# Moving the elimination steps of three of four 32x32 inverses from VectorE to GpSimd

## The chip, the cores and the metric

The kernel runs on one core of a Trainium2 chip. A core has a matrix engine (TensorE, "PE" in the profile, with its weight loads as "PEld"), VectorE ("DVE"), ScalarE ("ACT"), GpSimd ("POOL") and SyncE ("SP"), which here only issues DMAs. Each engine works through its own queue in order; semaphores tie the queues together. The metric is the device time of one execution in microseconds, as the median of several runs.

## The reference

A decoder trunk of two layers on 272 tokens (16 learned ones and 256 given) of width 2048, in float32. The first layer mixes tokens with RWKV-7, the second with gated linear attention; a squared-ReLU MLP follows each. The change lies in the RWKV-7 recurrence, which the reference computes token by token, for 32 heads with a 64x64 state each:

```python
def step(S, inp):
    r_t, w_t, k_t, v_t, a_t, b_t = inp
    sa = jnp.einsum('bhvk,bhk->bhv', S, a_t)
    S = S * w_t[:, :, None, :] + sa[..., None] * b_t[:, :, None, :] + v_t[..., None] * k_t[:, :, None, :]
    y = jnp.einsum('bhvk,bhk->bhv', S, r_t)
    return S, y
```

## The kernel before

Activations lie transposed, features on the partitions. Every matrix product with weights runs as three passes of TensorE on rounded parts of the float32 values: a weight block of 1024 columns is loaded by SyncE (`wload`, L140), rounded to `hi` by ScalarE (L149), and VectorE takes the difference `lo = raw - hi` (L150); `mm3` (L172 to L174) multiplies. In the recurrence `wload` works in two halves of 512 columns. Two sets of `hi` and `lo` are in use at a time.

The recurrence works in chunks: 4 of 64 tokens and a last one of 16 (padded to 32), for two groups `g` of 16 heads. Inside a chunk the tokens depend on each other through a unit triangular system per head. A 64x64 system is cut into two 32x32 diagonal blocks and the block between them; the diagonal blocks are inverted, and `merge` (L1101) joins two of them with two small products on TensorE (L1110 and L1120). `invert(b)` inverts the 32x32 blocks of half a group at once, one system to a partition: `b` = 0 and 1 for the chunks 0, 1 and then 2, 3, 4 of the first group, `b` = 2 and 3 the same for the second. So four inverses follow each other. The even ones use 64 partitions (2 chunks x 2 blocks x 16 heads), the odd ones 128 (partitions 64 to 95 are zeros).

The way of one inverse: `scores(b, c, e)` (L930) makes the systems on TensorE (L940), VectorE masks them on their way out of PSUM into `AM` (the helper `tt`, line L703), SyncE sends the blocks to `sysd` in HBM (L947) and reads them back into `sysA`, one system to a partition (L966). GpSimd fills the diagonal with ones (L967; for odd `b` L963 clears the idle partitions). Then come 30 steps, `s` = 1 to 30, each a product into the small tile `upd` of `s` rows by `31 - s` columns and a sum into `sysA`: 60 instructions on VectorE, each waiting for the one before. `upd` has one buffer. After them SyncE stores `sysA` into `invd` (L977) and reads it back into `AM` in the layout of the chunks (L984), and VectorE transposes it into the spare partitions 64 to 95 of `sysA` (L979), from where L1110 reads it. L1120 reads the blocks that L984 brings.

Four things set the order of work here. TensorE's order is written out by hand: inside `tc.manual_schedule(engines={ENG.PE})` it takes the instructions as the program gives them. `R(n)` puts n units (three or so matmuls) of the value and output projections between the pieces of the recurrence, `until(n)` as many as are missing to n in all, `GAPS` and `MARK` are tables of such numbers, and `some(inv, n)` advances the generator `invert` by n yields. Nothing in TensorE's order looks at whether an inverse is done; when its turn comes, a merge waits. The other engines' orders come from the framework's planner, which replays the program with costs of its own and fills each queue by due priority; `tc.high_priority` moves loads and the stores around the inverse forward. VectorE's queue holds, beside the steps, the splits L150, the masks of the scores, the group norm of the first group (`norm`, L1263 to L1266, during the third inverse) and the additions of projection results to `r` and `hres`. GpSimd's queue holds in this part of the kernel only the fills, the copies of `WC` (L1054) and the clearing of `uv` for the last chunk (L1139).

## Time and profile before

| | |
|---|---|
| median of 3 runs | 2339.26 us (2339.04 to 2339.55) |
| the profiled execution | 2338.97 us, its span 2337.2 us |
| granted TensorE clock | 0.998 |
| recurrence with the four inverses | about 258 to 485 us of the span |
| inverses (first step to last, on VectorE) | 258.3 to 302.5, 328.1 to 353.7, 389.9 to 424.9, 439.1 to 474.2 us |

The span is the time between the first and the last instruction of the program; the execution's own time has a start and an end around it. A row of an engine with an instruction gives its duration; a "wait" is idle time of an engine put down to what ended it. Helpers record all their instructions under their own line: each `tt` of the recurrence stands under L703, so rows are told apart by the tiles they write and read, and `upd` and `sysA` mark the inverse.

### The profile page before, as it was taken

To read this page: it belongs to the slowest core of one execution; us is meant where nothing else is said; L and a number is where in the kernel's file an instruction comes from. 1 tells how busy PE (TensorE), PEld (TensorE's weight loads), DVE (VectorE), ACT (ScalarE), POOL (GpSimd) and SP (SyncE) were. 2 spreads that over 40 slices of the span, in tenths; PEclk is the share of its full clock that TensorE was granted. 3 is DMA by queue.
4 is the path that set the end of the run, shared out by engine and by line. 5 is a ranking of instruction groups with operands and counts; after the bars stand their busy time and mean duration, and the time that the engine had idled before them with its cause. 6 is when DMAs were issued, how large, how long until landed. Compare 5 with 4: busy or idle time off the path is not lost.

```text
span 2337.2 us, 49049 instructions
## 1 busy us (share of the span) xinstructions
PE 2308.0 (99%) x19183; PEld 2175.8 (93%) x19183; DVE 1816.0 (78%) x2979; ACT 1378.0 (59%) x2167; POOL 301.4 (13%) x597
## 2 busy tenths in 40 slices
PE   9999999999999999999999999999999999999998
PEld 8888888889999999999999999999998888898987
DVE  8868986848677667767767787677768989989877
ACT  6488645556555445445445565455577777777766
POOL 0000000000144444444430011000000000000000
PEclk9999999999999999999999999999999999999999
DMA  6459754535799999999996665555557777877875
GB/s 213 161 193 310 246 169 141 153 90 172 257 314 334 314 318 325 325 323 320 330 319 227 198 227 199 175 174 182 209 196 263 272 271 265 274 266 265 274 267 188
DMA packets 200326, 567.75 MB, mean 243 GB/s; under 512 B 41184, under 2 KB 56800, under 8 KB 199968
## 3 DMA queue, kind: packets, MB, share of 16 engines
q1 hardware_dynamic: 173216, 476.53, 59.7%
q0 software_dynamic: 26880, 88.10, 12.1%
q8 instruction: 151, 2.47, 0.4%
q14 instruction: 79, 0.65, 0.1%
HBM read 504.38 MB, written 58.46 MB: 241 GB/s over the span
## 4 chain that ended last, share of the span: by engine, by line
PE 83%; DVE 10%; ACT 3%; issue 2%; DMA 1%; SPq 0%; DVEq 0%; ACTq 0%
PE pj L172 16%; PE pj L174 16%; PE pj L173 16%; PE pj L418 10%; PE pj L419 5%; PE pj L205 2%; DVE lo L150 2%; PE pj L206 1%; PE pu L498 1%; PE pu L500 1%; PE pu L499 1%; PE pt L500 1%; PE pt L498 1%; PE pt L499 1%; ACT hi L149 1%
## 5 line engine op out<-in xcount | busy, mean ns | idle before, releaser
L149 ACT CAST hi<-raw 128x1024 fp32r<-128x1024 f32 (+1 forms) x562 | 526.1, 947 | 593.9 <-PE pj L173 530.6
L150 DVE TENSOR_TENSOR lo<-raw,hi 128x1024 fp32r<-128x1024 f32 (+1 forms) x562 | 613.1, 1100 | 224.8 <-ACT hi L149 220.1
L172 PE MATMUL pj<-x,hi 128*128 128x272 f32 (+1 forms) x2560 | 728.4, 285 | 2.0 <-DVE r L703 0.9
L174 PE MATMUL pj<-x,lo 128*128 128x272 f32 (+1 forms) x2560 | 714.7, 279 | 4.4 <-DVE lo L150 4.1
L173 PE MATMUL pj<-x,hi 128*128 128x272 f32 (+1 forms) x2560 | 713.6, 279 | 0.0
L172 PEld LDWEIGHTS pj<-x,hi 128*128 128x128 f32 x2560 | 484.8, 189 | 14.8 <-issue 6.5
L174 PEld LDWEIGHTS pj<-x,lo 128*128 128x128 f32 x2560 | 484.9, 189 | 6.8 <-DVE lo L150 6.5
L173 PEld LDWEIGHTS pj<-x,hi 128*128 128x128 f32 x2560 | 485.0, 189 | 2.5 <-issue 1.4
L372 DVE TENSOR_TENSOR lo<-raw,hi 128x1024 fp32r<-128x1024 f32 x364 | 405.1, 1140 | 72.1 <-ACT hi L664 70.8
L664 ACT CAST hi<-raw 128x1024 fp32r<-128x1024 f32 x364 | 352.3, 981 | 112.6 <-PE pj L418 30.7
L418 PE MATMUL pj<-x,hi 128*128 128x512 f32 x1024 | 339.5, 383 | 0.0
L172 PE MATMUL pj<-h,hi 128*128 128x272 f32 x1024 | 285.7, 279 | 0.0
L173 PE MATMUL pj<-h,hi 128*128 128x272 f32 x1024 | 285.7, 279 | 0.0
L174 PE MATMUL pj<-h,lo 128*128 128x272 f32 x1024 | 285.7, 279 | 0.0
L419 PE MATMUL pj<-x,lo 128*128 128x256 f32 x1024 | 279.2, 273 | 0.0
L418 PEld LDWEIGHTS pj<-x,hi 128*128 128x128 f32 x1024 | 193.5, 189 | 26.7
L419 PEld LDWEIGHTS pj<-x,lo 128*128 128x128 f32 x1024 | 196.4, 192 | 1.9 <-DVE lo L372 0.2
L172 PEld LDWEIGHTS pj<-h,hi 128*128 128x128 f32 x1024 | 193.5, 189 | 0.0
L173 PEld LDWEIGHTS pj<-h,hi 128*128 128x128 f32 x1024 | 193.5, 189 | 0.0
L174 PEld LDWEIGHTS pj<-h,lo 128*128 128x128 f32 x1024 | 193.5, 189 | 0.0
L358 POOL DMA_DIRECT2D diff<-x x168 | 90.2, 543 | 14.3 <-DVE x L351 5.1
L344 POOL DMA_DIRECT2D x<-w_d x168 | 89.8, 540 | 0.3
(359 smaller groups left out, 3517.7 us busy)
## 6 DMA issues: line engine op xcount, KB each, us to landing
raw<-mlp_w_d SPq DMA_DIRECT2D x384, 512.0 KB, 6.1
raw<-gla_in_d SPq DMA_DIRECT2D x98, 512.0 KB, 3.3
x<-w_d POOLq DMA_DIRECT2D x168, 256.0 KB, 6.8
diff<-x POOLq DMA_DIRECT2D x168, 256.0 KB, 8.6
raw<-w_rkv_d SPq DMA_DIRECT2D x80, 512.0 KB, 3.9
raw<-w_d SPq DMA_DIRECT2D x69, 512.0 KB, 4.5
raw<-diff SPq DMA_DIRECT2D x55, 512.0 KB, 5.2
raw<-gla_o_d SPq DMA_DIRECT2D x32, 512.0 KB, 3.3
```

Of the source, the lines that this page charges most:

```text
L149: nc.scalar.copy(hi[:, h], raw[:, h])
L150: nc.vector.tensor_tensor(out=lo[:, h], in0=raw[:, h], in1=hi[:, h].bitcast(F32), op=ALU.subtract)
L172: nc.tensor.matmul(out, hi[:, ws], xh, start=first, stop=False)
L173: nc.tensor.matmul(out, hi[:, ws], xl, start=False, stop=False)
L174: nc.tensor.matmul(out, lo[:, ws], xh, start=False, stop=last)
L205: nc.tensor.matmul(wide, hi[:, ws], xt, start=kt == 0, stop=False)
L344: nc.gpsimd.dma_start(x[:, body], w[:, k])
L358: nc.gpsimd.dma_start(self.diff[b, g, i][:, k], x[:, body])
L372: tt = lambda o, a, b, op: nc.vector.tensor_tensor(out=o, in0=a, in1=b, op=op)
L418: nc.tensor.matmul(wide, hi[:, ws], xt, start=kt == 0, stop=False)
L419: nc.tensor.matmul(narrow, lo[:, ws], xt[:, 0], start=False, stop=kt == KT - 1)
L664: nc.scalar.copy(hi, raw)
```

## The change

The 60 instructions of the steps of an inverse are issued to the engine `eng`: GpSimd for `b` = 0, 2 and 3, VectorE for `b` = 1. The arithmetic and the tiles are the same. The fills, the transposes and all DMAs stay on their engines, and TensorE's written order is the same.

```diff
         def invert(b):
             X = sysA
-            n = P if b % 2 else 64
+            n, eng = P if b % 2 else 64, nc.vector if b == 1 else nc.gpsimd
             some_rows = [slice(0, 64), slice(96, 112)][: 1 + b % 2]
...
             for s in range(1, 31):
                 k, m = 31 - s, s
                 w = self.t(lp, [P, 240], "upd", 1)[:n, : k * m].rearrange("p (a b) -> p a b", a=m)
-                tt(w, X[:n, s : s + 1, s + 1 :].to_broadcast([n, m, k]), X[:n, :m, s : s + 1].to_broadcast([n, m, k]))
-                tt(X[:n, :m, s + 1 :], X[:n, :m, s + 1 :], w, ALU.add)
+                x = X[:n, :m, s + 1 :]
+                eng.tensor_tensor(out=w, in0=X[:n, s : s + 1, s + 1 :].to_broadcast([n, m, k]),
+                                  in1=X[:n, :m, s : s + 1].to_broadcast([n, m, k]), op=ALU.mult)
+                eng.tensor_tensor(out=x, in0=x, in1=w, op=ALU.add)
                 yield
```

In the changed kernel the steps stand under their own lines rather than under L703.

## The prediction

> **What bounds the kernel now.** I read the page first, then the waits of TensorE around the four inverses, then the inverses' own rows.

> ```profile
> span 2337.2 us, 49049 instructions
> ...
> PE 2308.0 (99%) x19183; PEld 2175.8 (93%) x19183; DVE 1816.0 (78%) x2979; ACT 1378.0 (59%) x2167; POOL 301.4 (13%) x597
> ```

> TensorE (PE) sets the end: it is busy 2308.0 of 2337.2 us. A change to VectorE work can therefore win only where TensorE stands still for VectorE, and lose wherever it makes TensorE wait longer. The next rows are the busy times in the stretches of the first, third and fourth inverse (columns: stretch, its length, then busy time of each engine), then the share of VectorE that is inverse steps (instructions that touch the tile upd).

> ```profile
> 258.30:303.00 44.70, 41.04 (x355) 37.97 (x353) 43.62 (x122) 23.77 (x49) 0.55 (x2) 1.00 0.72 236
> 389.90:426.70 36.80, 34.43 (x450) 29.34 (x445) 35.63 (x97) 17.29 (x37) 0.15 (x1) 1.00 0.46 136
> 435.30:476.70 41.40, 38.66 (x604) 33.42 (x602) 36.63 (x101) 25.86 (x52) 0.02 (x1) 1.00 0.45 138
> ...
> 258.30:303.00 44.70, 19.26 (x60) 1.00 0.72 236
> 389.90:425.00 35.10, 19.17 (x60) 1.00 0.47 139
> 435.30:474.20 38.90, 19.79 (x60) 1.00 0.45 139
> ```

> VectorE is nearly full there (43.62 of 44.70, 35.63 of 36.80, 36.63 of 41.40), and about half of it is the 60 instructions of one inverse. TensorE loses 3.7, 2.4 and 2.7 us. What it waits for, in the same three stretches:

> ```profile
> PE pj L174 <- DVE lo L150: 2.4, 2, 1.8
> PE pt L940 <- DVE AM L703: 2.4, 6, 0.6
> PE pj L172 <- DVE r L703: 0.9, 1, 0.9
> PE pj L172 <- DVE hres L703: 0.7, 1, 0.7
> ```

> The waits for VectorE are 2.4 + 2.4 + 1.6 = 6.4 us. That is all this change can win: 0.27% of the span. The rest of the idle time is for ScalarE, which is not touched.

> **What the change removes.** 180 VectorE instructions, 19.26 + 19.17 + 19.79 = 58.2 us of VectorE time, in just those three stretches. They add the same 180 on POOL, where the only neighbours in the queue are the fills of sysA and uv (L963, L967, L1139) and two of the small WC copies (L1054); no DMA is added or moved from its queue. Everything that follows an inverse now waits for POOL instead: the four transposes (L979) in VectorE's queue, with weight splits L150 queued behind them, and the store of sysA (L977) in SyncE's queue, with weight loads L140 behind it.

> **What a step costs on POOL.** No row shows a two-input operation on POOL. Its nearest rows:

> ```profile
> L1077 POOL MEMSET sysA<- 128x1024 f32 x1 | 1.0, 955 | 37.3 <-DVE ca L883 37.3
> L906 POOL MEMSET W<- 128x5 f32 x2 | 0.1, 107 | 0.0
> L349 POOL COPY x<-z 128x2 f32<-128x2 f32 x26 | 4.8, 184 | 176.6 <-DVE z L281 176.6
> L703 DVE TENSOR_TENSOR upd<-sysA x120: 182/342/410, 258.3 to 473.8; 64x30 f32<-64x30 f32 x4, 64x58 f32<-64x58 f32 x4, 64x84 f32<-64x84 f32 x4, 64x108 f32<-64x108 f32 x4
> ...
> 230.69 0.47 ACT L1036 ACTIVATE W<-hres 128x320 f32<-128x320 f32 x1 [0.85 <-DVE ar L703]
> ...
> 231.22 0.35 POOL L1054 COPY WC<-W 128x4 f32<-128x4 f32 x1 [7.23 <-ACT W L1036]
> ```

> Fixed part: a copy of two elements takes 184 ns, and a step depends on the one before it, so its whole latency counts. With 0.06 us to hand over (an estimate from the last two rows: ScalarE's W ends at 231.16, the WC copy starts at 231.22) that is 0.25 us, 60 x 0.25 = 14.8 us an inverse. Elements: the 30 steps have s x (31 - s) elements each, 4960 in all, twice (product and sum): 9920. Lower bound, the pace of the fill: (955 - 107) / 1019 = 0.83 ns, 8.2 us, so an inverse of 23 us. Upper bound: two reads and one write, each at that pace and in turn, 2.5 ns, with the 0.35 us of the WC copy as the fixed part: 24.8 + 60 x 0.41 = 49 us. Between them, two reads in turn at the fill's pace are 1.66 ns; and twice what VectorE takes for such a step, 2 x (410 - 182) / (240 - 30), is 2.17 ns. I take the middle of these two, 1.9 ns: 18.9 + 14.8 = **33.7 us** for an inverse that nothing disturbs.

> **What VectorE and POOL take from each other.** The two copies above differ by what VectorE does meanwhile. Three copies of POOL in a row, and VectorE under them:

> ```profile
> 630.62 1.97 POOL L343 COPY x<-z 128x2 f32<-128x2 f32 x3
> ...
> 630.72 0.70 DVE L350 TENSOR_TENSOR x<-x,x 128x513 f32<-128x513 f32 x1 [0.28 <-POOL x L349]
> 631.33 1.22 DVE L150 TENSOR_TENSOR lo<-raw,hi 128x1024 fp32r<-128x1024 f32 x1
> ```

> ```profile
> L150 DVE TENSOR_TENSOR lo<-raw,hi 128x512 fp32r<-128x512 f32 x9 | 5.8, 679 | 0.0
> L1263 DVE SCALAR_TENSOR_TENSOR ysq<-hres,vecs,ysq 128x272 f32<-128x272 f32 x4 | 2.0, 488 | 0.0
> L703 DVE TENSOR_TENSOR r<-r,ysq 128x272 f32<-128x272 f32 x4 | 1.7, 428 | 0.0
> L703 DVE TENSOR_TENSOR r<-r,hres 128x272 f32<-128x272 f32 x2 | 0.9, 427 | 0.0
> ```

> 10.4 us, about 9 without the 0.08 us by which such instructions overlap. In the fourth it is about 10; in the first 43.62 - 19.26 = 24.4 less some score evictions from PSUM, and what runs until 312 us: about 25. From these comes off what runs in POOL's handovers, 0.06 us for each: 3.6, 1.1 and 1.3.

> **When the results are due.** Start of each (POOL's diagonal fill L967), store of the result (L977), reload (L984), and the two halves of the merge on TensorE (L1110, L1120):

> ```profile
> 258.33 0.15 POOL L967 MEMSET sysA<- 64x32 f32 x1 [3.98 <-DMA sysA<-sysd]
> 302.79 0.48 SPq L977 DMA_DIRECT2D invd<-sysA  x1
> 309.42 1.51 SPq L984 DMA_DIRECT2D AM<-invd  x3
> 323.62 1.13 PE pt L1120 x64
> 389.97 0.15 POOL L967 MEMSET sysA<- 64x32 f32 x1 [7.87 <-DMA sysA<-sysd]
> 425.00 0.45 SPq L977 DMA_DIRECT2D invd<-sysA  x1
> 434.20 1.13 PE pt L1120 x64
> 435.16 0.16 POOL L967 MEMSET sysA<- 128x32 f32 x1 [1.53 <-issue]
> 474.28 1.08 SPq L977 DMA_DIRECT2D invd<-sysA  x2
> 479.20 0.49 SPq L984 DMA_DIRECT2D AM<-invd  x1
> 484.59 1.13 PE pt L1120 x64
> DMA to landing us min/median/max: 1.8/3.0/4.1
> ```

> The last reload is issued at 310.9 for the first, 479.7 for the fourth, and by the fourth's distance of 5.4 us behind the store at 430.4 for the third; with 3.0 us to land, L1120 has 9.7, 0.8 and 1.9 us to spare (first, third, fourth). So the store, which is issued as the last step ends, may go 9.7, 0.8 and 1.9 us later than now: 312.5, 425.8 and 476.2, or 54.0, 35.7 and 40.9 us behind the end of the diagonal fill.

> **The sum.** First: 33.7 + 25 - 3.6 = 55.1, 1.1 late. Third: 33.7 + 9 - 1.1 = 41.6, 5.9 late. Fourth: 33.7 + 10 - 1.3 = 42.4, 1.5 late. TensorE's order is written out by hand, so it stands at each merge; the next inverse begins behind that merge and moves with it, so the three add up: 8.5 us. The 6.4 us of waits that vanish lie ahead of these merges, where TensorE then only comes early to a wait that ends later; nothing of them comes off. 2337.2 + 8.5 = 2345.7 span; the profiled execution took 2338.97, 1.8 beyond its span and 0.3 under the median 2339.26, so I forecast **2348 us** against that median. What hides the rest: the first inverse has 9.7 us of cover; without it that term is 10.8 us, not 1.1.

> **The rivals.** (a) Everything hidden, **faster**: POOL's steps run near the fill's pace. An inverse is then 23 us, and with the disturbance 44, 31 and 32 against 54.0, 35.7 and 40.9: none late, and the 6.4 us come off, 2333. It decides from about 28 us an inverse downwards, where the third (35.7 due) is on time. For it speaks only that fill; against it, that a step reads two operands and the copies' 184 ns. (b) About even: 28 to 32 us an inverse; the third 0 to 4 late, first and fourth on time, with 4 us won there at 28 and under 1 at 32: 2335 to 2343. (c) Twice VectorE's pace to the full, 2.17 ns: 36.3 us, 2.6 more three times, 16.3 us late in all: 2356. [...] (d) The queues: the planner sets the place of the transposes in VectorE's order by its own idea of POOL's time. If it takes POOL for as fast as VectorE, they stay where they are (303 us), and VectorE stands there for 10 us or more with L150 behind them. Two sets of hi and lo cover 48 matmuls, at 41.04 / 355 us each 5.5 us of TensorE, so some 5 us are lost in the first, and 5 in each of the others on top of their lateness: 2363 and up. It decides once POOL is over 5 us behind plan. That the steps stay on VectorE is no rival; the engine is named in the code.

> **How the numbers follow.** Forecast (2343 to 2353): 0.30. (a) 0.27. (b) 0.21. (c) 0.14. (d) 0.08. The 8-in-10 range runs from (a) to between (c) and (d): 2332 to 2364; the forecast's own is 2343 to 2353. What a measurement can tell from no change here is about 0.2%, 4.7 us: 2334.6 to 2343.9. (a) is faster, 0.27; (b) and a tenth of the forecast's chance are the same, 0.24; the rest is slower, 0.49.

> **What would show it.** Right: POOL busy around 33 us more in each stretch, steps spaced 0.25 us plus 1.9 ns an element and longer where L150 runs; VectorE's L150 sometimes ending later than its 0.68 us; TensorE waiting at L1110 for L979 or at L1120 for L1123 and the reload, longest in the third inverse; the waits for AM and lo at L940 and L174 gone. Wrong: no wait at the merges and POOL's steps ended before 312.5, 425.8 and 476.2 us (then (a)); or TensorE waiting for lo at L174 with VectorE idle ahead of L979 (then (d)).

## The result, and the profile after

The changed kernel takes **2403.96 us** in the median (2401.95 to 2407.10) against 2339.41 of the kernel before on the same chip: 64.6 us or 2.8% slower, ratio 1.0276 with a 95% interval from 1.0258 to 1.0293. The forecast was 2348, in a range up to 2364: the sign was right, the size was not. In the changed kernel the steps are L973 and L975, the transposes L981, the store L979, the reload L986 and the two halves of the merge L1112 and L1122.

The page of the changed kernel: span, busy time of each engine, and the granted TensorE clock in 40 slices.

```profile
span 2401.6 us, 49035 instructions
...
PE 2314.7 (96%) x19183; PEld 2183.9 (91%) x19183; DVE 1778.4 (74%) x2799; ACT 1377.0 (57%) x2167; POOL 400.9 (17%) x777
...
PEclk9999899889999999999999999999999999999999
```

VectorE has 37.6 us less to do (1816.0 before), POOL 99.5 us more, and the span is 64.4 us longer. Three slices, in the stretch of the inverses, have a lower clock (0.88, 0.80 and 0.83). The waits of TensorE between 225 and 580 us of the changed kernel (total, times, longest):

```profile
PE pt L940 <- DVE AM L703: 23.0, 1, 23.0
PE pj L172 <- DVE hres L703: 20.7, 1, 20.7
PE pj L174 <- DVE lo L150: 20.2, 2, 17.1
...
PE pu L1009 <- DVE kn L1046: 0.6, 1, 0.6
```

Nearly the whole loss is in three waits of 17.1, 23.0 and 20.7 us, one for each inverse that was moved. Together with the 3.1 us of the second wait for lo and the 0.6 for kn, the waits for VectorE are 64.5 us, against 6.6 before (the 6.4 of the prediction and a wait of 0.2): 57.9 more. That is about all by which TensorE's idle time has grown, 57.7 us (2401.6 - 2314.7 = 86.9 against 2337.2 - 2308.0 = 29.2). Its busy time has grown by 6.7 (2314.7 against 2308.0), at the lower clock (0.985 in the mean against 0.998), and 57.7 + 6.7 are the 64.4. None of the waits is at a merge, where the forecast had put the loss. What VectorE and SyncE do around the first of them (two timelines of the changed kernel: start, length, instruction):

```profile
279.92 1.69 DVE L150 TENSOR_TENSOR lo<-raw,hi 128x512 fp32r<-128x512 f32 x2
281.53 0.88 DVE L703 TENSOR_TENSOR r<-r,hres 128x272 f32<-128x272 f32 x1
300.90 1.45 DVE L981 STREAM_TRANSPOSE sysA<-sysA 32x256 f32<-32x256 f32 x3 [18.49 <-POOL sysA L975]
302.38 1.29 DVE L150 TENSOR_TENSOR lo<-raw,hi 128x512 fp32r<-128x512 f32 x2
```

```profile
281.64 0.33 SPq L140 DMA_DIRECT2D raw<-w_rkv_d  x1
300.89 0.48 SPq L979 DMA_DIRECT2D invd<-sysA  x1
301.46 0.54 SPq L926 DMA_DIRECT2D AR<-ard  x1
```

VectorE comes to the transposes at 282.4 us, 24 us after the inverse began, and stands for 18.49 us until POOL's last step has ended at 300.9. The next weight split (L150) is queued behind them. SyncE stands just as long at the store of sysA, with the loads of weights and of AR behind it. Before, the store stood at 302.8 us and the transposes at 303.7, when the steps on VectorE had ended. The same happens at the other two inverses: VectorE comes to the transposes 15 and 14 us after they began, and stands for 21.2 and 22.2 us. All three places lie well before POOL's end, as if the planner took POOL's inverse for no longer than the 19.3 us of VectorE's steps; that is inferred from the places, no run shows its estimate. The stretches of the three stands (columns: stretch, length, busy time of PE, PEld, DVE, ACT and POOL, clock, DMA share, GB/s):

```profile
282.40:300.90 18.50, 3.61 (x32) 3.40 (x30) 0.01 (x2) 2.56 (x5) 16.04 (x32) 0.68 0.13 50
426.00:447.70 21.70, 1.38 (x8) 0.87 (x7) 0.51 (x2) 0.00 (x0) 18.89 (x36) 0.65 0.02 7
492.00:513.40 21.40, 3.91 (x29) 3.52 (x28) 0.00 (x0) 3.14 (x7) 18.64 (x36) 0.70 0.05 13
```

In 61.6 us, VectorE works 0.5, ScalarE 5.7 and TensorE 8.9: nearly everything stands, but POOL. So these stretches also show what POOL's steps cost when nothing disturbs them (groups of POOL instructions at the end of the third inverse, by shape; the mean in ns stands before the second bar, and 0.08 us pass before each next one):

```profile
L975 POOL TENSOR_TENSOR sysA<-sysA,upd 64x240 f32<-64x240 f32 x2 | 1.3, 660 | 0.2
...
L973 POOL TENSOR_TENSOR upd<-sysA 64x240 f32<-64x240 f32 x2 | 1.2, 606 | 0.2
...
L975 POOL TENSOR_TENSOR sysA<-sysA,upd 64x30 f32<-64x30 f32 x1 | 0.3, 256 | 0.1
L973 POOL TENSOR_TENSOR upd<-sysA 64x30 f32<-64x30 f32 x1 | 0.2, 244 | 0.1
```

An element costs (606 - 244) / 210 = 1.72 ns in the product and (660 - 256) / 210 = 1.92 ns in the sum; the forecast had 1.9. The second half of the fourth inverse, 30 instructions from 496.07 to 513.38 us, takes 17.3 us, and the two halves have the same shapes: 34.6 us for an inverse by itself, where the forecast had 33.7. POOL's price was not the mistake.

Last, the clock behind the first wait (same columns):

```profile
304.00:305.00 1.00, 1.00 (x6) 1.00 (x6) 0.97 (x3) 0.00 (x0) 0.00 (x0) 0.50 1.10 329
...
307.00:308.00 1.00, 1.00 (x11) 1.00 (x10) 0.07 (x1) 0.71 (x2) 0.00 (x0) 1.00 1.18 278
```

TensorE restarts at 303.13 us and runs at half clock, 6 matmuls to the microsecond instead of 11, until about 306. Such a stretch stands behind each of the four waits of 3 us and more, some 16 us at half clock in all (summed over windows of 1 us), which is enough for the 6.7 us.

### The profile page after: what moved, and what is told of

Same layout as the page of the kernel before. It is cut to its first block, busy times and chain, and to the rows that moved or that the text cites. A ratio compares the mean times of both kernels' runs of the same rounds, so it can differ in the third digit from the quotient of the medians.

```text
span 2401.6 us, 49035 instructions
## 1 busy us (share of the span) xinstructions
PE 2314.7 (96%) x19183; PEld 2183.9 (91%) x19183; DVE 1778.4 (74%) x2799; ACT 1377.0 (57%) x2167; POOL 400.9 (17%) x777
## 3 DMA queue, kind: packets, MB, share of 16 engines
q1 hardware_dynamic: 173216, 476.53, 58.2%
## 4 chain that ended last, share of the span: by engine, by line
PE 76%; DVE 1%; ACT 1%; issue 0%; DMA 0%; DVEq 0%; ACTq 0%
PE pj L172 15%; PE pj L173 14%; PE pj L174 14%; PE pj L418 9%; PE pj L419 5%; PE pj L205 2%; PE pj L206 1%; PE pu L498 1%; PE pu L499 1%; PE pu L500 1%; PE pt L500 1%; PE pt L499 1%; PE pt L498 1%; PE pj L499 1%; PE pj L500 1%; PE pj L498 1%
## 5 line engine op out<-in xcount | busy, mean ns | idle before, releaser
L150 DVE TENSOR_TENSOR lo<-raw,hi 128x1024 fp32r<-128x1024 f32 (+1 forms) x562 | 616.8, 1107 | 250.4 <-ACT hi L149 245.7
L172 PE MATMUL pj<-x,hi 128*128 128x272 f32 (+1 forms) x2560 | 732.5, 286 | 21.9 <-DVE hres L703 20.7
L174 PE MATMUL pj<-x,lo 128*128 128x272 f32 (+1 forms) x2560 | 718.6, 281 | 22.3 <-DVE lo L150 22.0
L172 PEld LDWEIGHTS pj<-x,hi 128*128 128x128 f32 x2560 | 488.7, 191 | 34.6 <-DVE hres L703 20.9
L174 PEld LDWEIGHTS pj<-x,lo 128*128 128x128 f32 x2560 | 489.0, 191 | 24.3 <-DVE lo L150 23.9
L172 PE MATMUL pj<-h,hi 128*128 128x272 f32 x1024 | 286.2, 280 | 0.0
L174 PE MATMUL pj<-h,lo 128*128 128x272 f32 x1024 | 286.2, 280 | 0.0
L174 PEld LDWEIGHTS pj<-h,lo 128*128 128x128 f32 x1024 | 194.1, 190 | 0.0
L172 PEld LDWEIGHTS pj<-h,hi 128*128 128x128 f32 x1024 | 194.1, 190 | 0.0
```

The lines of the kernel that those rows point to most:

```text
L150: nc.vector.tensor_tensor(out=lo[:, h], in0=raw[:, h], in1=hi[:, h].bitcast(F32), op=ALU.subtract)
L172: nc.tensor.matmul(out, hi[:, ws], xh, start=first, stop=False)
L174: nc.tensor.matmul(out, lo[:, ws], xh, start=False, stop=last)
```

## The experiments

**One inverse alone.** Theory Q (queues): each moved inverse makes its own stand. Only the first is left on POOL:

```diff
-            n, eng = P if b % 2 else 64, nc.vector if b == 1 else nc.gpsimd
+            n, eng = P if b % 2 else 64, nc.gpsimd if b in (0,) else nc.vector
```

> Only the first inverse is on POOL. Theory Q (order of the queues): the transposes stand in VectorE's queue, and the store of the result in SyncE's, where the planner puts POOL's end, some 20 us before POOL is done; TensorE loses the 3.1 + 17.1 us of the changed kernel's first inverse and wins back the 2.4 us of waits for lo: 2339 + 18 = 2357 us, the stall just before POOL's last step. Theory L (POOL's steps are too long for the merge, the sum of the prediction): the first is 1.1 us late, 2340 us. Theory P (POOL's reading of SBUF holds VectorE back so far that VectorE is the bound): some 20 us too, but spread over many small waits for lo.

Measured: 2362.76 us (2362.47 to 2363.05), ratio 1.0100 (1.0080 to 1.0121). TensorE's waits of this kernel between 225 and 580 us hold the same 17.1 us:

```profile
PE pj L174 <- DVE lo L150: 20.2, 2, 17.1
```

So one inverse costs about 23.7 us, and the first one costs it although it has 9.7 us to spare at its merge. That is 5.8 more than theory Q said: it counted the waits alone, and TensorE's busy time is 5.7 us longer as well (2313.7 against 2308.0).

**The places in the two queues.** Three kernels keep the three inverses on POOL and change the order alone. The transposes are pinned in VectorE's queue behind the masking or the addition that TensorE's order has reached shortly before the merge, the store in SyncE's queue behind the last store of a system; each of the two, or both:

```diff
+            while b in held_back:
+                yield
             for rows in some_rows:
-                with tc.high_priority(offset=4000):
+                with tc.high_priority(offset=4000), behind(b, "sp"):
                     nc.sync.dma_start(invd[b][rows], X[rows])
             for k in (slice(8 * i, 8 * i + 8) for i in range(4)):
-                nc.vector.transpose(...)
+                with behind(b, "dve"):
+                    nc.vector.transpose(...)
```

Both placed late:

> All three inverses on POOL as in the changed kernel, but the four transposes are queued on VectorE, and the store on SyncE, behind instructions that come about when POOL is done: the score masks of the third score unit (first inverse), the last addition to r before the merge (third), the last addition of a projection before the merge (fourth). Q: the three stalls of 17 to 23 us go; what is left is what POOL's length costs at the merges: first none, third about 3 us, fourth 0 to 2, less the waits won: 2337 to 2346 us. L: the same as the changed kernel, about 2404, as POOL's steps take as long. P: above 2380, since POOL's reads are the same.

Measured: 2350.12 us (2349.11 to 2354.13), ratio 1.0051 (1.0034 to 1.0067). Of 64.6 us, 53.5 were the queues; the 11.1 that are left are more than theory Q allowed (2346 at most). Only the transposes placed late:

> As the late queues, but only VectorE's: the transposes are late, the store stands in SyncE's queue where the planner puts it. If VectorE's queue alone makes the stall: as with both late, 2337 to 2346. If SyncE's queue makes it alike, since the weight loads stand behind the store: VectorE runs on until the three raw buffers are used up, some 8 us of TensorE less the two sets of hi and lo that it had already: TensorE still stands about 10 us for each of the three, 2365 to 2385.

Measured: 2389.51 us, ratio 1.0215 (1.0194 to 1.0235), above the range of the expectation. Only the store placed late:

> The other half: only the store is late, the transposes stand in VectorE's queue where the planner puts them. Q with VectorE's queue as the cause: TensorE stands as long as in the changed kernel, 2398 to 2405. If SyncE's queue were the cause: 2337 to 2350.

Measured: 2395.40 us, ratio 1.0240 (1.0219 to 1.0260), a little under the range. TensorE's waits with the transposes alone placed late, and then with the store alone (added code has moved the lines by 2 and more: the split is L152 now, the helper L705, the scores L942, the products of the projections L174 to L176):

```profile
PE pu L1267 <- DMA g<-g_d: 18.9, 1, 18.9
PE pt L942 <- DMA AR<-ard: 14.8, 2, 14.4
```

```profile
PE pj L176 <- DVE lo L152: 21.0, 2, 18.0
PE pt L942 <- DVE AM L705: 21.0, 1, 21.0
PE pu L1199 <- DVE S L705: 12.2, 1, 12.2
```

Each queue by itself makes most of the loss. With VectorE free, TensorE waits 18.9 and 14.4 us for loads (g, AR) that stand behind the store in SyncE's queue; with SyncE free, it waits for VectorE as in the changed kernel. The gains of 14.5 and 8.6 us do not add up to 53.5, because at the first and the third inverse either stand is enough. At the fourth it takes VectorE's: with the transposes alone placed late, SyncE stood there too, from 497.4 to 517.8 us, and TensorE still worked 19.0 of the 21 us around it.

**What is left: the places, or POOL?** With both placed late, 11.1 us were still lost. TensorE's waits in that kernel:

```profile
PE pj L174 <- DVE hres L705: 4.5, 3, 2.1
PE pj L176 <- DVE lo L152: 3.1, 1, 3.1
PE pt L1122 <- DVE sysA L991: 2.8, 1, 2.8
PE pt L942 <- DVE AM L705: 2.2, 2, 1.8
```

The waits for lo, AM and hres that the change was to remove are still there, although VectorE no longer has the steps; L1122 is the first half of the merge and L991 the transposes. Three theories: POOL's reads slow VectorE down (blocking), POOL's inverse is too long whatever VectorE does (length), or my places cost something by themselves. The first control has all inverses on VectorE and keeps the late places:

> All four inverses on VectorE as before; only the late places of the transposes and of the store are kept (first, third and fourth inverse). It shows what the placing costs by itself. If what was left of the loss with both placed late (2350.1 against 2339.0) comes from POOL, this is the kernel before again: 2336 to 2342. If the placing made part of it, 2344 or more.

Measured: 2346.45 us (2345.51 to 2349.14) against 2340.42 before, ratio 1.0027 (1.0016 to 1.0038). Two of its waits:

```profile
PE pt L1122 <- DVE sysA L991: 2.8, 1, 2.8
PE pj L174 <- DVE hres L705: 2.5, 2, 1.8
```

So about half of what was left came from my own pins: the wait for sysA is the same 2.8 us with POOL and without. In the third and fourth inverse I had put them behind additions that end 2.6 and 5.9 us after POOL's last step. At the same places, the steps left out:

> The 180 steps of the first, third and fourth inverse are left out altogether, on any engine (so those systems are not inverted); transposes and store placed late. It is the most that any engine could win by taking these steps off VectorE. My sum says that VectorE's lateness costs TensorE 6.4 us: 2333, within 2331 to 2336. If VectorE is late for another reason, 2337 to 2341.

Measured: 2340.64 us, ratio 1.0002 (0.9993 to 1.0011), 5.8 us under the control; the forecast of 2333 missed the pins' cost. And fills instead of steps:

> Placed late as before, but POOL fills each step's output twice (two fills of 240 elements: 2 x (0.107 + 0.83 x 0.235) = 0.60 us, about as long as a step of 240 elements, 0.6 to 0.67) in place of multiplying and adding: POOL is busy as long, but reads nothing (those systems are not inverted). Blocking theory (POOL's reads lengthen VectorE's two-input work: L152's halves took 0.89 us against 0.68): the halves are back at 0.68 and the time is near that without steps, 2333 to 2338. Length theory (an inverse of 36 us is simply late at the merges, whatever VectorE does): L152 plays no part, 2341 to 2350.

Measured: 2337.25 us, ratio 0.9985 (0.9976 to 0.9994). This one doesn't decide: the fills of upd wait for nothing and ran ahead of their inverse (operation, count, min/median/max in ns, first and last start):

```profile
L986 POOL MEMSET upd<- x180: 114/246/304, 159.2 to 385.2; 64x30 f32 x8, 64x58 f32 x8, 64x84 f32 x8, 64x108 f32 x8
```

The first began at 159.2 us, 100 us before the inverse, so POOL was busy within an inverse for only half as long as meant. The first inverse alone on POOL, placed late:

> Only the first inverse on POOL, its transposes and its store placed late; third and fourth on VectorE as before. It has 9.7 us to spare at its merge. Length theory: on time, the two waits for lo there (2.4 us) vanish: 2336 to 2338, the best version with this change in it. Blocking theory: VectorE's work before the merge is longer by as much as the steps freed (28 halves by 0.2 us, the two-input additions by 0.15 to 0.25), a wait for lo of some 3 us and a slower clock behind it: 2339 to 2344.

Measured: 2341.32 us (2339.78 to 2345.28), ratio 1.0006 (0.9996 to 1.0015). No measurable difference, and no gain: its waits for lo are 3.7 us, where they were 2.4 before. The length theory has no reason for this, since the first inverse was on time.

**The same four with places that cost nothing.** The transposes of the third inverse go behind an earlier weight split, those of the fourth behind an update of S; the fills are all of sysA, so that they follow on one another:

```diff
+            if queue == 'dve' and b > 1:
+                return tc.issue_after((self.los[-2] if b == 2 else last['S']).ins)
...
+                else:
+                    for y in (x, x, x, x):
+                        nc.gpsimd.memset(y, 0.0)
```

> All inverses on VectorE; first inverse placed late as before, but the transposes of the third stand one weight split earlier and those of the fourth right behind an update of S, so that they no longer wait for something that comes after POOL's end. The late places of the last runs cost 6.0 us (2346.5 against 2340.4) with waits of 2.8 us for sysA and 1.8 us for hres. If those two waits, and the slower clock behind them, were that cost: 2338 to 2342. If something else in the placing was: 2344 to 2347.

Measured: 2339.49 us, ratio 0.9995 (0.9986 to 1.0004): the places are free now.

> The same places, the 180 steps of the first, third and fourth inverse left out (those systems are not inverted): the most that any engine could win by taking them off VectorE. My sum's 6.4 us under the kernel before: 2332 to 2335. With the other places this was 5.8 us under the steps on VectorE.

Measured: 2332.08 us (2331.10 to 2332.94), ratio 0.9963 (0.9948 to 0.9978). With these places and this order of TensorE it is the ceiling: 7.4 us under the steps on VectorE.

> The same places; POOL writes each step's elements of sysA four times with zeros instead of multiplying and adding (those systems are not inverted). All four fills follow on one another within the inverse (in the run before, the half of them that wrote upd ran ahead of the inverse, so POOL was busy for half as long as meant). Four fills of 240 elements, 4 x 0.30 = 1.2 us with 0.06 to 0.08 between them, against two steps of 0.6 to 0.67: the inverse lasts about 36 to 40 us, as with the real steps, and reads nothing. Blocking theory: L152's halves at 0.68 us, TensorE late only by what the third inverse passes 35.7 us: 2333 to 2340. Length theory: as late as with the real steps, 2342 to 2348.

Measured: 2333.95 us (2331.18 to 2336.39), ratio 0.9971 (0.9960 to 0.9981). The inverses lasted 34.8, 34.8 and 35.6 us on POOL (from 259.1, 387.1 and 432.1), as long as the real steps take undisturbed, and cost 1.9 us over none at all, which the two intervals can't tell from nothing.

> The same places, the three inverses on POOL: the change with both queues seen to and no wait of the placing's own. 2350.1 with the other places; less 4 to 6 us: 2343 to 2347 if POOL's reads are what is left (5 us over the steps on VectorE at the same places); 2334 to 2340 if the placing was all of it.

Measured: 2346.77 us (2342.89 to 2348.43), ratio 1.0025 (1.0015 to 1.0035): 7.3 us over the same kernel with the steps on VectorE, 12.8 over the fills, 14.7 over none. Blocking it is: inverses that keep POOL busy as long as the undisturbed steps, but read nothing, cost next to nothing. VectorE's busy time over the whole kernel is 1789.4 us beside the steps and 1766.6 beside the fills, 22.8 more for the same instructions. Its weight splits in the stretch of the first inverse, 258 to 304 us, first beside the fills and then beside the real steps (count, busy us and mean ns, then idle before):

```profile
L152 DVE TENSOR_TENSOR lo<-raw,hi 128x512 fp32r<-128x512 f32 x24 | 15.5, 687 | 11.1 <-ACT hi L151 11.1
```

```profile
L152 DVE TENSOR_TENSOR lo<-raw,hi 128x512 fp32r<-128x512 f32 x22 | 20.7, 980 | 4.4 <-PE pt L943 4.1 <-ACT hi L151 0.2
L706 DVE TENSOR_TENSOR r<-r,hres 128x272 f32<-128x272 f32 x4 | 3.2, 810 | 0.0
```

A split of 512 elements takes 0.687 us beside fills, as before the change (0.679 in the prediction's row), and 0.980 beside steps that read; an addition of 272 elements 0.810 instead of 0.43. POOL is held up in turn: its three inverses last 48.2, 39.8 and 38.4 us there, against 34.6 alone. The score masks, which take one of their two inputs from PSUM, were not lengthened: 0.676 us beside the steps, 0.683 beside the fills. The 12.8 us hold both sides of the blocking, VectorE's and POOL's, and no run parts them. TensorE's waits in the kernel with the real steps:

```profile
PE pj L177 <- DVE lo L152: 3.6, 2, 3.1
PE pt L943 <- DVE AM L706: 2.6, 2, 1.8
PE pt L1135 <- ACT hi L151: 2.1, 1, 2.1
PE pj L175 <- DVE hres L706: 1.9, 2, 1.4
PE pt L1270 <- DVE hres L1281: 0.9, 1, 0.9
...
PE pt L1125 <- DVE sysA L994: 0.3, 1, 0.3
```

Against the kernel before, the span is 7.7 us longer (2344.9): 2.4 at the third merge (L1125 and L1135), 2.4 in the waits for VectorE (3.6 + 2.6 + 1.9 + 0.9 = 9.0, where 6.6 were before), 3.0 in TensorE's busy time (2311.0 against 2308.0). The profile puts the 2.1 us at L1135, the second half of the merge, down to ScalarE's hi, which that product does not read; beside the fills the same wait, 1.6 us, is put down to the reload. Nor is SyncE's queue quite free in this kernel: it stands at the store for 5.7 us in the third inverse and 17.8 in the fourth (5.2 and 3.3 beside the fills). No wait of TensorE for a load shows there, but a cost of these stands is not excluded.

No version with the change beats the kernel before. The nearest is the first inverse alone with its transposes and store placed late, and it is even.

## Why the prediction was wrong

**What bounds the kernel, and the 6.4 us:** right. Without the 180 steps the kernel is 7.4 us faster than with them at the same places. That is all this change could have won.

**What a step costs on POOL:** right within 3% (34.6 us measured, 33.7 forecast). Rival (c), twice VectorE's pace to the full, is too dear: 36.3. Its 2.17 ns an element lies above both measured paces, 1.72 and 1.92.

**What VectorE and POOL take from each other:** the assumption that VectorE is held up by POOL's reads as POOL is by VectorE's was right, and the fills show it (a split of 512 elements takes 0.687 us beside them, 0.980 beside the steps). The lengths it gave for the disturbed inverses were 55.1, 41.6 and 42.4 us; with the places mended they are 48.2, 39.8 and 38.4. So POOL was lengthened by 13.6, 5.2 and 3.8 us over its 34.6, where the prediction added 21.4, 7.9 and 8.7: the term was over-sized. And it was only counted as lateness of POOL. That the weight splits themselves take 0.98 instead of 0.68 us, and that TensorE waits for them ahead of the merges, has no term in the sum; "the 6.4 us of waits that vanish" did not vanish, they became 9.0.

**When the results are due:** the third inverse was the only late one, as the due times say (39.8 against 35.7), and cost 2.4 us at its merge; the sum had 5.9 there and 8.5 over the three.

**The sum:** here is the step that failed. The paragraph on what the change removes said that "everything that follows an inverse now waits for POOL instead: the four transposes (L979) in VectorE's queue, with weight splits L150 queued behind them, and the store of sysA (L977) in SyncE's queue, with weight loads L140 behind it". Then the sum gave these waits no price: it let VectorE and SyncE go on until POOL was done, and looked for the loss at the merges only. VectorE took its instructions in order (at the first stand the next split began at 302.38 us, behind the transposes of 300.90), so that holds only with the transposes at the right place. They stood 24, 15 and 14 us after the inverse's start, and POOL needed 42, 36 and 37. About 57 of the 64.6 us are this step: 2403.96 against 2346.77 with the places mended.

**Rival (d), the queues,** was this mechanism and had a chance of 0.08. Its sign to look for, TensorE waiting for lo at L174 with VectorE idle ahead of the transposes, is the first stand to the letter. Its price, "2363 and up", was too low by 40 us for these reasons. It left the transposes at 303 us, where the steps on VectorE had ended between 20 us of other work; in the changed kernel they stand well before POOL's end, at 282 us in the first (that the planner moved them to where it thinks the steps end is inferred). It took the stand for 10 us or more; it is 18.5 to 22.2. And it deducted 5.5 us of cover from two sets of hi and lo; VectorE stood for 61.9 us (18.5 + 21.2 + 22.2) and TensorE waited 60.8 (17.1 + 23.0 + 20.7). And no term had the half clock behind each stand.

**Rivals (a) and (b)** fell with the step's price. By its own number, the forecast of 2348 is close to the 2346.77 of the kernel with free places, but by another road (2.4 us at the merges, not 8.5), so that is no support for its sum.

## What to carry to other kernels

When work moves to a slower engine, look first at who consumes its result, in which queue the consumer stands, and what stands behind it: here the wait of one consumer became a stand of its whole engine (18.5, 21.2 and 22.2 us on VectorE), and each of two queues alone made most of the loss. Then ask whether the two engines can run side by side at all: VectorE was rid of 58 us of steps, and what it had left took 22.8 us longer beside POOL's reading steps than beside fills, so that no gain remained. The ceiling of such a change can be measured at once by leaving the work out (here 7.4 us of 2339), before any engine is tried.

## What the runs showed of the hardware

POOL's fills left VectorE's two-input subtraction at 0.687 us, POOL's two-input steps brought it to 0.980; POOL being busy was not enough, the instructions that lengthened it were those that read. That the effect goes both ways shows best in the shortest step, 30 elements (timeline of POOL in the kernel with both placed late):

```profile
257.39 1.54 POOL L980 TENSOR_TENSOR upd<-sysA 64x30 f32<-64x30 f32 x1
...
392.20 0.23 POOL L980 TENSOR_TENSOR upd<-sysA 64x30 f32<-64x30 f32 x1
```

0.23 us alone, and 1.54 us in the first inverse, beside VectorE's two-input work. In the changed kernel the same step took 1.06 us, from 258.58 to 259.64 us: a split of 1024 elements had begun 0.60 us before it and ended at 259.20, and the two-input operation behind that split (`kk` from `sq` and `kk`) ended at 259.55.

The half clock after a wait is not decided by its length alone. In the same kernel a wait of 3.1 us for lo is followed by 4.6 us at half clock (columns: stretch, length, busy time of TensorE, clock, DMA share, GB/s):

```profile
277.80:282.40 4.60, 4.60 (x20) 0.50 0.56 149
```

and with the mended places a wait of 3.1 us for lo at nearly the same point is followed by a full clock (here with the busy times of all engines):

```profile
278.00:282.50 4.50, 4.50 (x39) 4.50 (x40) 4.50 (x6) 1.14 (x2) 4.11 (x6) 1.00 0.56 151
```

20 matmuls there, 39 here. What decides between the two, no run here shows. By the 4.6 us at half clock, the price of such a wait is uncertain by some 2 us, an estimate.
